# Weight scaling cut into slices on two engines, v stored in blocks, and two reorderings around the output projection of a gMLP and attention trunk

## The chip, the cores and the metric

The kernel runs on one core of a Trainium2 chip. The metric is the device time of one launch in microseconds; lower is better. TensorE (PE) multiplies, VectorE (DVE), ScalarE (ACT) and GpSimd (POOL) work elementwise, and SyncE (SP) issues most of the DMA transfers. ScalarE issues some too. Each engine takes its instructions strictly in order, and so does each engine's queue of DMA issues.

## The reference

The input x is 1024 tokens by 1024 channels in float32. Layer one is a gated MLP with a spatial gate, layer two a banded attention with sinks; both have a residual and a norm on each side.

```python
# layer one (gmlp_mixer), h = rms_norm(x, a_pre_g)
u, v, z = split(h @ w_in, 3)              # each 1024 x 2048
u = gelu(u); v = layer_norm(gelu(v), ln_g, ln_b)
s = einsum('gts,bnsgc->bntgc', tril(w_s), v) + b_s     # 8 groups, chunks of 128 tokens
y = (u * s * silu(z)) @ w_out             # 2048 -> 1024
h1 = x + rms_norm(y, a_post_g)
k, v = rms_norm(h1, kv_norm_g) @ w_k, ... @ w_v        # shared, 4 heads of 64
# layer two (swa_mixer), h = rms_norm(h1, b_pre_g)
q, z = split(h @ b_w_in, 2)               # 16 heads of 64
o = softmax(q k^T + alibi, sliding window 128, sink) v
out = h1 + rms_norm((o * silu(z)) @ b_w_out, b_post_g)
```

## The kernel before

Every large product is taken as three matmuls of 128x128 by 128x512 on operands split in a high and a low part: hi*hi, hi*lo and lo*hi (`mm3`, the profile's lines L174 to L176). `split` (L104) makes the parts: ScalarE copies the high part (L105), VectorE subtracts it (L106). So each weight or activation piece passes ScalarE and then VectorE before TensorE can take it.

The stages follow one another on TensorE, in this order and at these times of the span: `v_layer` (0 to some 163 us; steps m = 1, 2, 5, 6, 7, 4, 3 for two halves Q of the columns, banks vb and vc), `uz_layer` (to 482; banks ub, uc, ua, the spatial gate from vg and wc), `out_layer` (to 658; seven products m, four steps u each, banks ob and oc), `q_phase` of token half 0 (to 702), `kv_phase` (to 725), `z_phase` of half 0 (to 775), attention of half 0 (to 905), and the other half with the last projection. The first three layers use a scheme of seven products for a 2x2 block product, so a bank is added to several results and some are reused: in `out_layer` the bank oc takes m=5 and, right behind it, m=3.

The code is written as Python generators; a `side` generator is advanced by `step(side)` between groups of matmuls, so that norms and transposes run beside the matmuls. The order in which instructions are issued within an engine is then set by a scheduler that starts from the order written. What a table of orders shows below is the result.

The parts that the change touches:
- `Weights.split` (L133) prepares the 40 weight tiles of layer two, each 128x1024. The 16 of kind "q" (w_q and w_z of the first half) are first multiplied by the gain b_pre_g, in place, by one GpSimd instruction over the whole tile (L144); then split, and the scaled tile is written back to DRAM by ScalarE's queue (`wsc`, L151), from where the second half reads it without scaling.
- `v_layer` applies GELU to each 128x512 tile of v (`done`, L387) and `emit` (L381) takes its statistics on VectorE and stores the tile, 256 KB, to `vd` in DRAM, one store issued by ScalarE behind each activation.
- `out_layer` (L767): at the end of a product m each of the four token tiles t is summed with the bank (`add`, L211, yoa<-yoa,oc), and `done` (L844) takes its sum of squares on ScalarE (junk_oa, L188) and multiplies it by the gain a_post_g on VectorE (yoa<-yoa,gpa).
- `norm_h1` (L747) norms a half of layer one's output, h1, for layer two: tile hb = h1 * r (L755), eight transposes to the banks nt (L761), split into n_hi and n_lo. For half 0 it takes yo, the tiles on chip, as a side of m=5 and m=3; for half 1 it loads h1 back from DRAM (`h1d`), four loads of 512 KB on SP, as a side of `z_phase`.
- `group_consts` (L575), unchanged, loads wc and bsb for the spatial gate of each of eight groups on SP's queue; the matmul rb (L585) needs wc, after GpSimd's affine_select (L583) has masked it.

Of the kernel before, what the change touches and what calls it, by code (L numbers as in the profile page):

```python
# [34 lines left out]
def step(*gens):  # L35
    for g in gens:
        next(g, None)
# [7 lines left out]
def drain(g):  # L45
    for _ in g:
        pass
# [3 lines left out]
def tile_yoco(  # L51
# [63 lines left out]
    class Weights:  # L115
# [17 lines left out]
        def split(self, i):  # L133
            while len(self.done) <= min(i, len(self.order) - 1):
                n = len(self.done)
                self.load(n)
                raw, (src, kind, back) = self.raw[n], self.order[n]
                hi = wpool.tile([P, 1024], F32R, tag="whi", name=f"whi{n}")
                lo = wpool.tile([P, 1024], F32R, tag="wlo", name=f"wlo{n}")
                halves = [slice(kk * 512, kk * 512 + 512) for kk in range(2)]  # L140
                if kind == "q":
                    rv = raw.rearrange("p (k c) -> p k c", k=KT)
                    g = gn[:, G_BPRE:G_BPRE + KT].unsqueeze(2).broadcast_to([P, KT, P])
                    nc.gpsimd.tensor_tensor(rv, rv, g, ALU.mult)  # L144
                if kind[:2] == "kv":
                    for kk, cs in enumerate(halves):
                        split_scaled(hi[:, cs], lo[:, cs], raw[:, cs], gain(G_KV, 2 * int(kind[2:]) + kk))
                else:
                    split(hi, lo, raw)
                if back is not None:  # L150
                    nc.scalar.dma_start(out=back, in_=raw)  # L151
                self.done.append((hi, lo))
# [10 lines left out]
    def gain(c, k):  # L163
        return gn[:, c + k:c + k + 1]
# [25 lines left out]
    def load_tok(src, name):  # L190
        t = st.tile([P, D], F32, tag="xt", name=name)
        nc.sync.dma_start(out=t, in_=src)
        return t
# [100 lines left out]
    def v_layer(ahead):  # L294
# [83 lines left out]

        stats = vp.tile([P, NB, 4, 6], F32, name="bst")

        def emit(slot_, i, j, t, Q):  # L381
            qd = 2 * Q + i
            nc.vector.bn_stats(stats[:, 4 * j + t, qd], slot_)
            nc.scalar.dma_start(out=vd[4 * j + t, :, qd * 512:(qd + 1) * 512], in_=slot_)

        def done(out, src, i, j, t, Q):
            nc.scalar.activation(out, src, AF.Gelu_apprx_tanh, scale=rx[j][:, t:t + 1])  # L387
            emit(out, i, j, t, Q)

        ORDER = (1, 2, 5, 6, 7, 4, 3)  # L390
        steps = [(Q, m, u) for Q in range(2) for m in ORDER for u in range(2)]
# [42 lines left out]
        for n, (Q, m, u) in enumerate(steps):  # L434
            if u == 0:
                if m == 1:
                    bank_b = [bank("mm", f"vb{Q}_{t}") for t in range(4)]
                elif m in (2, 5):
                    bank_c = [bank("s", f"vc{Q}{m}_{t}") for t in range(4)]
            ps = bank_b if m in (1, 6, 7, 4) else bank_c  # L440
            first = m in (1, 2, 5)
            hi, lo = ready.pop(n)
            for kk in range(2):
                k = 2 * u + kk
                cs = slice(kk * 512, kk * 512 + 512)
                for t in range(4):
                    ts_ = slice(t * P, (t + 1) * P)
                    mm3(ps[t], T[m][0][:, k, ts_], T[m][1][:, k, ts_], hi[:, cs], lo[:, cs],
                        first and k == 0, k == HT - 1)
            if n >= 2:  # L450
                prep(n + 2)
            if n >= len(steps) - 3:
                step(ahead)
            if n == 0:
                xload(xa[:, 1], 0, 1, 0, 2)
            elif n == 1:
                prep(3)
                xload(xa[:, 1], 0, 1, 2, 2)
            elif n >= 4:
                step(side)  # L460
            if u == 0:
                continue
            for t in range(4):
                if m == 1:
                    a1.append(slots[0][:, t])
                    copy(a1[t], ps[t])
                elif m == 2:
                    add(a1[t], a1[t], ps[t], ALU.add)
                    if Q:
                        done(a1[t], a1[t], 0, 0, t, Q)  # L470
                elif m == 6:
                    if t == 0:
                        e6 = big.tile([P, 4, TH], F32, tag="P1_3", name=f"ve6_{Q}")
                    copy(e6[:, t], ps[t])
                elif m == 7:
                    e67.append(slots[1][:, t])
                    copy(e67[t], ps[t])
                    add(e67[t], e67[t], bank_c[t], ALU.add)
                    if Q:
                        done(e67[t], e67[t], 1, 1, t, Q)  # L480
                elif m == 4:
                    c = slots[Q][:, t]
                    done(c, ps[t], 1, 0, t, Q)
                elif m == 3:
                    add(e6[:, t], e6[:, t], ps[t], ALU.add)
                    done(e6[:, t], e6[:, t], 0, 1, t, Q)

            late = {6: (a1, 0), 4: (e67, 1)}.get(m) if Q == 0 else None
            if late:
                for t in range(4):  # L490
                    done(late[0][t], late[0][t], late[1], late[1], t, Q)
            if m == 3:
                a1, e67 = [], []
            if Q == 1 and m == 2:
                broadcast_rstd()
# [248 lines left out]
        rstd(r1[h], s1, f"h1{h}")  # L744
        yield

    def norm_h1(h, n, yo=None):  # L747
        for t in range(4):
            if yo is None:
                xt = load_tok(h1d[h][t], f"hb{h}_{t}")  # L750
                src = xt
            else:
                xt = st.tile([P, D], F32, tag="xt", name=f"hb{h}_{t}")
                src = yo[t]
            nc.vector.tensor_scalar(xt, src, r1[h][:, t:t + 1], None, ALU.mult)  # L755
            yield
            for kq in range(2):
                ps = bank("s", f"nt{h}_{t}_{kq}").rearrange("p (k t) -> p k t", k=4)
                for k in range(4):
                    c = (kq * 4 + k) * P  # L760
                    nc.tensor.transpose(ps[:, k], xt[:, c:c + P], ident)  # L761
                sl = (slice(None), slice(kq * 4, kq * 4 + 4), slice(t * P, (t + 1) * P))
                split(n[0][sl], n[1][sl], ps)
            yield


    def out_layer():  # L767
# [84 lines left out]
        for n, (m, u) in enumerate(steps):  # L852
# [12 lines left out]
            for kk in range(2):  # L865
                cs = slice(kk * 512, kk * 512 + 512)
                k = 2 * u + kk
                for t in range(4):
                    ts_ = slice(kk * 512 + t * P, kk * 512 + (t + 1) * P)
                    mm3(ps[t], thi[:, ts_], tlo[:, ts_], shi[:, cs], slo[:, cs],  # L870
                        m in (1, 2, 5) and k == 0, k == 7)
                step(side)
            if u < 3:
                prep(n + 2)
                continue
            for t in range(4):
                if m == 1:
                    if t == 0:
                        yo[0] = yo_alloc((0, 1), "yoa0")
                    copy(yo[0][t][:, half[0]], ps[t])  # L880
                elif m == 2:
                    dst = yo[0][t][:, half[0]]
                    add(dst, dst, ps[t], ALU.add)
                    done(t, 0, 0, dst)
                elif m == 6:
                    if t == 0:
                        yo[1] = yo_alloc((2, 3), "yoa1")
                    copy(yo[1][t][:, half[0]], ps[t])
                elif m == 7:
                    copy(yo[1][t][:, half[1]], ps[t])  # L890
                elif m == 4:
                    evac_out(yo[0][t], ss[0], ps[t], t, 1, gp, "oa10")
                elif m == 5:
                    dst = yo[1][t][:, half[1]]
                    add(dst, dst, ps[t], ALU.add)
                    done(t, 1, 1, dst)
                else:
                    dst = yo[1][t][:, half[0]]
                    add(dst, dst, ps[t], ALU.add)
                    done(t, 0, 1, dst)  # L900
            prep(n + 2)
            if m == 4:
                n0 = pair("P3", "n0")
                side = chain(chain_a(0, yo[0], ss[0], xs), iter(range(2)), norm_h1(0, n0, yo[0]))
# [270 lines left out]
    for _ in main:  # L1175
        step(side)
    drain(side)
    gp = post_gain(b_post, "gpb")
    drain(kv_phase(0, n0))
    n1 = pair("P2", "n1")  # L1180
    z0, z1 = ([big.tile([P, 4, TH], F32, tag=f"P1_{2 * i}", name=f"z{h}_{i}") for i in range(2)]
              for h in range(NH))
    side = norm_h1(1, n1)
    for _ in z_phase(0, n0, z0, 0, 8):
        step(side)
    drain(side)
# [74 lines left out]
```

## Time and profile before

| | before |
|---|---|
| median of 3 runs | 1063.02 us (1061.49 to 1063.05) |
| the profiled execution | 1062.77 us |
| its span | 1061.1 us |
| TensorE busy | 1045.5 us, 5114 matmuls |
| VectorE / ScalarE / GpSimd busy | 739.6 / 569.5 / 233.0 us |
| DMA moved | 168.08 MB |

Rows of the profile read as follows. A row of the timeline begins with its start and its length in us; then come the engine, the line, the operation, output<-inputs with the buffer numbers left out, shapes, a count, and in brackets the idle time ahead of it on its engine and what ended it. ACTq and SPq are the issuing of transfers. A row of the waits tells who waited for whom: us in total, how many times, the longest. A row of a group has the busy time and the mean ns of one, then the idle time ahead of the group and its releasers. A DMA row ends in the median us from issue to landing. A 128x512 matmul is listed with 0.39 us, but the next starts 0.23 us later, since they overlap.

### The profile page before, as it was taken

How to read it: one execution, taken by the hardware profiler on the slowest of the kernel's cores; microseconds unless marked ns; L12 is line 12 of the kernel's file. 1: busy time of each engine (PE TensorE's matmuls, PEld its weight loads, DVE VectorE, ACT ScalarE, POOL GpSimd, SP SyncE). 2: the span in 40 equal slices, each digit the busy share in tenths (PEclk: the TensorE clock that was granted, in tenths of full speed). 3: DMA queues.
4: the chain of work that ended last, by engine and by line, in shares of the span. 5: the costliest groups of instructions: out<-in, count | busy, mean ns of one | idle time of the engine just before them, and what ended most of it. 6: DMA issues, size and time to landing. Idle time of an engine off the chain costs nothing.

```text
span 1061.1 us, 14120 instructions
## 1 busy us (share of the span) xinstructions
PE 1045.5 (99%) x5114; PEld 857.0 (81%) x5114; DVE 739.6 (70%) x1292; ACT 569.5 (54%) x973; POOL 233.0 (22%) x197
## 2 busy tenths in 40 slices
PE   9999999999999999999999989999999999999997
PEld 7887788888888888888888878788887777777776
DVE  6987466867767768678696586755357885667963
ACT  6674454555564555464444463544456665766631
POOL 0000003254253442540100121303101111122320
PEclk9999999999999999999999999999999999999999
DMA  8777252434333434348997643846522112111353
GB/s 311 265 276 262 99 177 91 131 112 135 115 109 129 139 103 132 115 141 281 344 331 255 218 159 129 288 152 219 175 72 71 62 61 80 61 60 61 120 179 119
DMA packets 70871, 168.08 MB, mean 158 GB/s; under 512 B 6417, under 2 KB 16913, under 8 KB 70801
## 3 DMA queue, kind: packets, MB, share of 16 engines
q1 hardware_dynamic: 63456, 150.04, 41.6%
q10 hardware_dynamic: 7344, 17.14, 4.3%
q8 instruction: 40, 0.66, 0.2%
q14 instruction: 31, 0.25, 0.1%
HBM read 127.31 MB, written 39.85 MB: 158 GB/s over the span
## 4 chain that ended last, share of the span: by engine, by line
PE 84%; DVE 6%; ACT 3%; DMA 3%; issue 2%; POOL 1%; ACTq 0%; DVEq 0%; POOLq 0%; SPq 0%
PE ub L174 5%; PE ub L176 5%; PE ub L175 5%; PE ob L174 5%; PE ob L176 5%; PE ob L175 5%; PE qz L174 5%; PE qz L176 5%; PE qz L175 5%; PE uc L175 3%; PE uc L174 3%; PE uc L176 3%; PE sp L602 3%; PE vb L175 2%; PE vb L176 2%
## 5 line engine op out<-in xcount | busy, mean ns | idle before, releaser
L174 PE MATMUL qz<-n_hi,whi 128*128 128x512 f32 x256 | 102.1, 399 | 0.4 <-DVE kl L994 0.2
L176 PE MATMUL qz<-n_hi,wlo 128*128 128x512 f32 x256 | 100.1, 391 | 1.1 <-DVE wlo L106 1.1
L175 PE MATMUL qz<-n_lo,whi 128*128 128x512 f32 x256 | 99.7, 390 | 0.0
L106 DVE TENSOR_TENSOR wlo<-raw_w,whi 128x1024 fp32r<-128x1024 f32 x40 | 51.7, 1292 | 42.9 <-ACT whi L105 30.1
L144 POOL TENSOR_TENSOR raw_w<-raw_w,gn 128x1024 f32<-128x1024 f32 x16 | 35.4, 2215 | 189.9 <-DMA raw_w<-in_wqz_dram 172.0
L1040 ACT ACTIVATE pr<-pr,mx 128x129 f32<-128x129 f32 x128 | 50.0, 393 | 36.4 <-DVE mx L1035 36.4
L105 ACT ACTIVATE whi<-raw_w 128x1024 fp32r<-128x1024 f32 x40 | 42.3, 1057 | 41.2 <-PE qz L175 19.7
L105 ACT ACTIVATE uzhilo_g<-f 128x1024 fp32r<-128x1024 f32 x31 | 32.8, 1060 | 48.0 <-PE uc L176 43.0
L176 PEld LDWEIGHTS qz<-n_hi,wlo 128*128 128x128 f32 x256 | 48.0, 188 | 12.2 <-DVE wlo L106 1.8
L174 PEld LDWEIGHTS qz<-n_hi,whi 128*128 128x128 f32 x256 | 48.1, 188 | 10.4 <-issue 0.8
L1059 POOL TENSOR_SCALAR_AFFINE_SELECT pp<-pc 128x512 f32<-128x512 f32 x28 | 20.5, 733 | 163.4 <-ACT pc L1056 163.4
L175 PEld LDWEIGHTS qz<-n_lo,whi 128*128 128x128 f32 x256 | 48.2, 188 | 9.4
L214 ACT ACTIVATE uz_slots<-ub 128x512 f32<-128x512 f32 x48 | 28.4, 591 | 43.6 <-PE ub L176 41.5
L106 DVE TENSOR_TENSOR uzhilo_g<-f,uzhilo_g 128x1024 fp32r<-128x1024 f32 x31 | 38.6, 1246 | 18.7 <-ACT uzhilo_g L105 18.6
L174 PE MATMUL ub<-T,whi_g 128*128 128x512 f32 x128 | 50.6, 396 | 0.0
L174 PE MATMUL ub<-T,uzhilo_g 128*128 128x512 f32 x128 | 50.5, 394 | 0.0
L176 PE MATMUL ub<-T,wlo_g 128*128 128x512 f32 x128 | 49.9, 390 | 0.0
L176 PE MATMUL ub<-T,uzhilo_g 128*128 128x512 f32 x128 | 49.9, 390 | 0.0
L175 PE MATMUL ub<-T,uzhilo_g 128*128 128x512 f32 x128 | 49.8, 389 | 0.0
L175 PE MATMUL ub<-T,whi_g 128*128 128x512 f32 x128 | 49.8, 389 | 0.0
L174 PE MATMUL uc<-T,uzhilo_g 128*128 128x512 f32 x124 | 48.9, 395 | 0.0
L175 PE MATMUL uc<-T,uzhilo_g 128*128 128x512 f32 x124 | 48.3, 389 | 0.0
(328 smaller groups left out, 3158.3 us busy)
## 6 DMA issues: line engine op xcount, KB each, us to landing
raw_uz<-in_wuz_in_dram SPq DMA_DIRECT2D x32, 512.0 KB, 3.5
td<-uz_slots SPq DMA_DIRECT2D x56, 256.0 KB, 2.1
orawP2a<-td SPq DMA_DIRECT2D x28, 512.0 KB, 4.1
raw<-in_wv_in_dram SPq DMA_DIRECT2D x17, 512.0 KB, 5.2
vg<-vd SPq DMA_DIRECT2D x8, 1024.0 KB, 5.4
orawP2b<-in_wo_a_dram SPq DMA_DIRECT2D x16, 512.0 KB, 8.0
raw_w<-in_wqz_dram SPq DMA_DIRECT2D x16, 512.0 KB, 4.2
wsc<-raw_w ACTq DMA_DIRECT2D x16, 512.0 KB, 3.0
```

Source lines behind the costliest of these rows:

```text
L105: nc.scalar.activation(hi, src, AF.Copy)
L106: nc.vector.tensor_tensor(lo, src, hi.bitcast(F32), ALU.subtract)
L144: nc.gpsimd.tensor_tensor(rv, rv, g, ALU.mult)
L174: nc.tensor.matmul(out, lhsT=a_hi, rhs=b_hi, start=start, stop=False, skip_group_check=True)
L175: nc.tensor.matmul(out, lhsT=a_hi, rhs=b_lo, start=False, stop=False, skip_group_check=True)
L176: nc.tensor.matmul(out, lhsT=a_lo, rhs=b_hi, start=False, stop=stop, skip_group_check=True)
L214: nc.scalar.activation(out, a, AF.Copy)
L602: nc.tensor.matmul(psv[:, n], lhsT=d["vg"][:, 4 * j + n, i * P:(i + 1) * P], rhs=d["wc"], start=True, stop=True)
L1040: nc.scalar.activation(pr[:, i], pr[:, i], AF.Exp, bias=mx[:, i // 2, i % 2:i % 2 + 1], scale=-1.0, accum_out=dn[:, i // 2, i % 2:i % 2 + 1])
L1059: nc.gpsimd.affine_select(self.pp, pc, [[0, 4], [-1, P]], ALU.is_ge, 0.0, base=-1, channel_multiplier=1)
```

## The change

Four edits.
1. The 16 weight tiles of kind "q" are scaled in eight slices of 128x128, each by its own column of gains: two slices on ScalarE (new line L146), six on GpSimd (L148).
2. A block of four token tiles of v is stored by one transfer of 1 MB instead of four of 256 KB, issued behind all four activations: 8 stores instead of 32, on the same queue.
3. In `out_layer` the four sums of m=5 are written ahead of their squares and products by gpa, and the last advance of the side generator in a product's last step comes after the evacuation, not before it (twice then, so that the number stays).
4. `norm_h1` of half 1 takes the tiles on chip like half 0, starts in the q phase of half 0 and goes on in `z_phase`; the four loads from `h1d` are gone, and the tile pair n1 is taken earlier. The stores to `h1d` stay, since the last residual reads them.

```diff
 # Weights.split
-                    g = gn[:, G_BPRE:G_BPRE + KT].unsqueeze(2).broadcast_to([P, KT, P])
-                    nc.gpsimd.tensor_tensor(rv, rv, g, ALU.mult)
+                    for k in range(KT):
+                        g = gain(G_BPRE, k)
+                        if k < 2:
+                            nc.scalar.activation(rv[:, k], rv[:, k], AF.Copy, scale=g)
+                        else:
+                            nc.gpsimd.tensor_scalar(rv[:, k], rv[:, k], g, None, ALU.mult)
 # v_layer
-        def emit(slot_, i, j, t, Q):
-            qd = 2 * Q + i
-            nc.vector.bn_stats(stats[:, 4 * j + t, qd], slot_)
-            nc.scalar.dma_start(out=vd[4 * j + t, :, qd * 512:(qd + 1) * 512], in_=slot_)
+        def store(block, i, j, Q):
+            dst = vd[4 * j:4 * j + 4, :, (2 * Q + i) * 512:(2 * Q + i + 1) * 512]
+            nc.scalar.dma_start(out=dst.rearrange("n p c -> p n c"), in_=block)
 
         def done(out, src, i, j, t, Q):
             nc.scalar.activation(out, src, AF.Gelu_apprx_tanh, scale=rx[j][:, t:t + 1])
-            emit(out, i, j, t, Q)
+            nc.vector.bn_stats(stats[:, 4 * j + t, 2 * Q + i], out)
...
+            block = {3: (e6, 0, 1), 4: (slots[Q], 1, 0)}.get(m)
+            if Q and m in (2, 7):
+                block = (slots[0], 0, 0) if m == 2 else (slots[1], 1, 1)
+            if block:
+                store(*block, Q)
...
                 for t in range(4):
                     done(late[0][t], late[0][t], late[1], late[1], t, Q)
+                store(slots[late[1]], late[1], late[1], Q)
 # norm_h1
-    def norm_h1(h, n, yo=None):
+    def norm_h1(h, n, yo):
         for t in range(4):
-            if yo is None:
-                xt = load_tok(h1d[h][t], f"hb{h}_{t}")
-                src = xt
-            else:
-                xt = st.tile([P, D], F32, tag="xt", name=f"hb{h}_{t}")
-                src = yo[t]
-            nc.vector.tensor_scalar(xt, src, r1[h][:, t:t + 1], None, ALU.mult)
+            xt = st.tile([P, D], F32, tag="xt", name=f"hb{h}_{t}")
+            nc.vector.tensor_scalar(xt, yo[t], r1[h][:, t:t + 1], None, ALU.mult)
 # out_layer
-                step(side)
+                if u < 3:
+                    step(side)
...
                     dst = yo[1][t][:, half[1]]
                     add(dst, dst, ps[t], ALU.add)
-                    done(t, 1, 1, dst)
...
             prep(n + 2)
+            if m == 5:
+                for t in range(4):
+                    done(t, 1, 1, yo[1][t][:, half[1]])
+            step(side, side)
 # behind the q phase of half 0
+    n1 = pair("P2", "n1")
+    side = norm_h1(1, n1, yo)
+    step(side)
     drain(kv_phase(0, n0))
-    n1 = pair("P2", "n1")
...
-    side = norm_h1(1, n1)
```

Lines behind the first edit move by 4, those behind `v_layer`'s by 10. The new order at three places, where a name's first part is the tile and the number behind it its serial:

SP's queue at the end of `v_layer`, where the loads for the first quads of `uz_layer` (raw_uz) and the constants of group 0 (vg, wc, bsb) go out; before:

```order
L101 DMA raw_uz_0_1364<-in_wuz_in_dram 128x1024
L578 DMA vg_1351<-vd 128x8x256
L101 DMA raw_uz_1_1366<-in_wuz_in_dram 128x1024
L580 DMA wc_1353<-in_ws_t_dram 128x128
L582 DMA bsb_1355<-in_bs_dram 128x128
L580 DMA wc_1631<-in_ws_t_dram 128x128
```

and with the change:

```order
L101 DMA raw_uz_0_1340<-in_wuz_in_dram 128x1024
L588 DMA vg_1327<-vd 128x8x256
L101 DMA raw_uz_1_1342<-in_wuz_in_dram 128x1024
L101 DMA raw_uz_0_1427<-in_wuz_in_dram 128x1024
L590 DMA wc_1329<-in_ws_t_dram 128x128
L592 DMA bsb_1331<-in_bs_dram 128x128
```

The third load of a raw_uz_0 has moved ahead of wc and bsb; its buffer is free when VectorE has split the piece wlo_g_1 of the load before it.

VectorE between m=5 and m=3, where yoa_2 holds token tiles 0 and 1 and yoa_3 tiles 2 and 3, oc_0 to oc_3 are the four banks, and gpa is the gain; before:

```order
L211 TENSOR_TENSOR yoa_2_4305<-yoa_2_4305,oc_0_4606 128x512
L211 TENSOR_TENSOR yoa_2_4305<-yoa_2_4305,oc_1_4607 128x512
L211 TENSOR_TENSOR yoa_3_4306<-yoa_3_4306,oc_2_4608 128x512
L211 TENSOR_TENSOR yoa_2_4305<-yoa_2_4305,gpa 128x512 x2
L211 TENSOR_TENSOR yoa_3_4306<-yoa_3_4306,oc_3_4609 128x512
L211 TENSOR_TENSOR yoa_3_4306<-yoa_3_4306,gpa 128x512
```

and with the change:

```order
L215 TENSOR_TENSOR yoa_2_4281<-yoa_2_4281,oc_0_4582 128x512
L215 TENSOR_TENSOR yoa_2_4281<-yoa_2_4281,oc_1_4583 128x512
L215 TENSOR_TENSOR yoa_3_4282<-yoa_3_4282,oc_2_4584 128x512
L215 TENSOR_TENSOR yoa_2_4281<-yoa_2_4281,gpa 128x512
L215 TENSOR_TENSOR yoa_3_4282<-yoa_3_4282,oc_3_4585 128x512
L215 TENSOR_TENSOR yoa_2_4281<-yoa_2_4281,gpa 128x512
L215 TENSOR_TENSOR yoa_3_4282<-yoa_3_4282,gpa 128x512
```

The fourth sum (oc_3) has moved ahead of the second product by gpa, not of the first.

TensorE around the end of m=3, where nt_3 are the transposes of token tile 3 of half 0 and qz_0_0 the first q product; before:

```order
L174 MATMUL oc_3_4609<-ohiloP0b,ohiloP0a 128x512
L175 MATMUL oc_3_4609<-ohiloP0b,ohiloP0a 128x512
L176 MATMUL oc_3_4609<-ohiloP0b,ohiloP0a 128x512
L761 MATMUL nt_3_0_4929<-ident,hb_3_4915 128x128 x4
L761 MATMUL nt_3_1_4936<-ident,hb_3_4915 128x128 x4
L174 MATMUL oc_0_4606<-ohiloP0b,ohiloP0a 128x512
L175 MATMUL oc_0_4606<-ohiloP0b,ohiloP0a 128x512
L176 MATMUL oc_0_4606<-ohiloP0b,ohiloP0a 128x512
```

and, further on there, up to the q phase:

```order
L175 MATMUL oc_2_4608<-ohiloP0b,ohiloP0a 128x512
L176 MATMUL oc_2_4608<-ohiloP0b,ohiloP0a 128x512
L174 MATMUL oc_3_4609<-ohiloP0b,ohiloP0a 128x512
L175 MATMUL oc_3_4609<-ohiloP0b,ohiloP0a 128x512
L176 MATMUL oc_3_4609<-ohiloP0b,ohiloP0a 128x512
L174 MATMUL qz_0_0_5006<-n_hi,whi_4992 128x512
L175 MATMUL qz_0_0_5006<-n_lo,whi_4992 128x512
L176 MATMUL qz_0_0_5006<-n_hi,wlo_4993 128x512
```

With the change:

```order
L180 MATMUL oc_2_4584<-ohiloP0b,ohiloP0a 128x512
L178 MATMUL oc_3_4585<-ohiloP0b,ohiloP0a 128x512
L179 MATMUL oc_3_4585<-ohiloP0b,ohiloP0a 128x512
L180 MATMUL oc_3_4585<-ohiloP0b,ohiloP0a 128x512
L766 MATMUL nt_3_0_4933<-ident,hb_3_4891 128x128 x4
L766 MATMUL nt_3_1_4940<-ident,hb_3_4891 128x128 x4
L178 MATMUL qz_0_0_4996<-n_hi,whi_4968 128x512
L178 MATMUL qz_0_1_5057<-n_hi,whi_4981 128x512
L179 MATMUL qz_0_0_4996<-n_lo,whi_4968 128x512
L180 MATMUL qz_0_0_4996<-n_hi,wlo_4969 128x512
```

The transposes have moved behind the last oc matmul, right ahead of the first matmuls that read the n_hi and n_lo made from them. A matmul of the second q product has come between.

ScalarE at the same place, where whi is a weight's high part, wsc_3 the store of the next scaled weight, and junk_oa the squares; before:

```order
L105 ACTIVATE whi_4992<-raw_w_4871 128x1024
L105 ACTIVATE n_hi<-nt_2_0_4889 128x4x128
L105 ACTIVATE n_hi<-nt_2_1_4896 128x4x128
L105 ACTIVATE whi_4998<-raw_w_4873 128x1024
L151 DMA wsc_3_91<-raw_w_5004 128x1024
L105 ACTIVATE n_hi<-nt_3_0_4929 128x4x128
L105 ACTIVATE n_hi<-nt_3_1_4936 128x4x128
L188 ACTIVATE junk_oa_0_4956,ssa_3859<-yoa_2_4305 128x512
L151 DMA wsc_4_92<-raw_w_5058 128x1024
L188 ACTIVATE junk_oa_1_4960,ssa_3859<-yoa_2_4305 128x512
```

and with the change:

```order
L105 ACTIVATE n_hi<-nt_2_1_4872 128x4x128
L146 ACTIVATE raw_w_4994<-raw_w_4994,gn 128x128 x2
L155 DMA wsc_3_91<-raw_w_4994 128x1024
L105 ACTIVATE whi_4981<-raw_w_4849 128x1024
L192 ACTIVATE junk_oa_0_4918,ssa_3835<-yoa_2_4281 128x512
L192 ACTIVATE junk_oa_1_4922,ssa_3835<-yoa_2_4281 128x512
L105 ACTIVATE n_hi<-nt_3_0_4933 128x4x128
L192 ACTIVATE junk_oa_2_4926,ssa_3835<-yoa_3_4282 128x512
L105 ACTIVATE n_hi<-nt_3_1_4940 128x4x128
L146 ACTIVATE raw_w_5055<-raw_w_5055,gn 128x128
L192 ACTIVATE junk_oa_3_4930,ssa_3835<-yoa_3_4282 128x512
```

The two slices and wsc_3 now stand ahead of whi_4981, and n_hi of tile 3 behind two squares. On VectorE all four sums and three of the four products by gpa stand ahead of the first n_lo<-nt_3.

## The prediction

> **What bounds the kernel now.** I read the busy table first, then the waits of TensorE, then the timeline around each wait. The page's head:
>
> ```profile
> span 1061.1 us, 14120 instructions
> PE 1045.5 (99%) x5114; PEld 857.0 (81%) x5114; DVE 739.6 (70%) x1292; ACT 569.5 (54%) x973; POOL 233.0 (22%) x197
> PEclk9999999999999999999999999999999999999999
> ```
>
> TensorE is busy for 99% of the span at a full granted clock. The change gives it the same matmuls in another order, so only its idle time can shrink or grow. The waits of TensorE (who, for whom: total us, times, longest):
>
> ```profile
> PE oc L174 <- DVE yoa L211: 2.8, 2, 1.9
> PE nt L761 <- DVE hb L755: 1.4, 1, 1.4
> PE qz L176 <- DVE wlo L106: 1.1, 1, 1.1
> PE vb L175 <- DVE vlo L106: 0.8, 1, 0.8
> ```
>
> That is 6.1 us, and the other rows of the view are the start-up and 0.4 or less each. What the change can win is therefore at most these 6.1; what it can lose has no such bound. The profiled execution took 1062.77 us, 0.25 under the median of 1063.02; the sum is made against the former.
>
> **Stores of v in blocks.** In v_layer's step m=4 ScalarE issues each 256 KB store between two activations:
>
> ```profile
> 79.73 1.68 ACTq L384 DMA_DIRECT2D vd<-vslot  x2
> 81.47 1.06 ACT L105 ACTIVATE vhi<-vraw 128x1024 fp32r<-128x1024 f32 x1 [1.14 <-issue]
> 83.88 1.07 PE L174 MATMUL vb<-vhi,T 128*128 128x512 f32 x4
> 83.24 1.26 DVE L211 TENSOR_TENSOR ve<-ve,vc 128x512 f32<-128x512 f32 x2
> 84.43 1.22 DVE L106 TENSOR_TENSOR vlo<-vraw,vhi 128x1024 fp32r<-128x1024 f32 x1
> ```
>
> Two issues take 1.68 there, and vhi starts late behind them. One issue per four tiles moves vhi to about 80, and VectorE's new order puts vlo ahead of the sums with vc: vlo can end between 81 and 83.7, and TensorE, one matmul every 0.23 us, wants it after its four of 83.88, at 84.8. **-0.8**. A slot of 1 MB comes free later than four of 256 KB; that could hold ScalarE for a microsecond or two at 150, where TensorE has no wait in 100 us. Nothing.
>
> **Order at uz_layer's start.** SP's order now puts the load raw_uz_0, which needs the piece that VectorE splits at the end of v_layer, ahead of group 0's wc:
>
> ```profile
> 156.62 0.47 SPq L580 DMA_DIRECT2D wc<-in_ws_t_dram  x1
> wc<-in_ws_t_dram SPq DMA_DIRECT2D x2, 64.0 KB, 3.7
> wc<-in_ws_t_dram SPq DMA_DIRECT2D x8, 64.0 KB, 5.2
> 166.93 0.17 DVE L498 TENSOR_SCALAR ve<-mv 128x8 f32<-128x8 f32 x1
> 167.17 1.64 POOL L499 TENSOR_TENSOR ve<-ve,small 128x8 f32<-128x8 f32 x1 [1.52 <-DVE ve L498]
> 168.78 0.64 POOL L583 TENSOR_SCALAR_AFFINE_SELECT wc<-wc 128x128 f32<-128x128 f32 x2
> 169.69 0.38 PE L585 MATMUL rb<-wc,ones 128*128 128x128 f32 x2
> ```
>
> Before, wc went out at 156.6 and lay ready nine us before rb. Now the piece wlo_g_1, which stands about where ve<-mv does, ends near 167.1, wc goes out at 167.5 and lands 3.7 later (the first two here) or 5.2 (median of all eight), at 171.2 to 172.7; affine_select 0.3. TensorE reaches rb ten matmuls (2.3 us) later in its new order and 0.9 earlier by the gain above: 171.0. **+0.5**, bounds 0 and 2.
>
> **Sums of the reused bank in out_layer, m=5 to m=3, and the slices there.**
>
> ```profile
> 627.55 3.95 POOL L144 TENSOR_TENSOR raw_w<-raw_w,gn 128x1024 f32<-128x1024 f32 x1 [3.79 <-DMA raw_w<-in_wqz_dram]
> 628.52 1.22 DVE L106 TENSOR_TENSOR wlo_s<-scho,whi_s 128x1024 fp32r<-128x1024 f32 x1
> 629.66 1.87 DVE L211 TENSOR_TENSOR yoa<-yoa,oc 128x512 f32<-128x512 f32 x3
> 631.53 0.33 ACTq L151 DMA_DIRECT2D wsc<-raw_w  x1
> 631.96 0.63 ACT L188 ACTIVATE junk_oa<-yoa 128x512 bf16<-128x512 f32 x1 [5.97 <-DVE yoa L211]
> 632.71 1.45 DVE L211 TENSOR_TENSOR yoa<-yoa,gpa 128x512 f32<-128x512 f32 x2 [1.18 <-ACT junk_oa L188]
> 634.08 0.68 DVE L211 TENSOR_TENSOR yoa<-yoa,oc 128x512 f32<-128x512 f32 x1
> ```
>
> The reading is a chain: POOL's scaling ends at 631.50, only then does ScalarE issue the store wsc, then the squares (junk_oa) of tile 0 and 1, then VectorE multiplies both by gpa, and only then comes the fourth sum (634.08), for which TensorE waits 1.9. The new order does not do all that its words say: one product by gpa still stands ahead of the fourth sum. It removes one, 0.7. What a slice costs no row shows; the nearest:
>
> ```profile
> L583 POOL TENSOR_SCALAR_AFFINE_SELECT wc<-wc 128x128 f32<-128x128 f32 x8 | 2.4, 306 | 12.3 <-PE ub L176 7.9 <-DMA wc<-in_ws_t_dram 4.5
> L211 POOL TENSOR_TENSOR f<-raw_uz,raw_uz 128x512 f32<-128x512 f32 x15 | 19.2, 1282 | 125.6 <-DVE uzhilo_g L106 125.6
> L1040 ACT ACTIVATE pr<-pr,mx 128x129 f32<-128x129 f32 x128 | 50.0, 393 | 36.4 <-DVE mx L1035 36.4
> 651.72 1.90 POOL L144 TENSOR_TENSOR raw_w<-raw_w,gn 128x1024 f32<-128x1024 f32 x1 [20.22 <-DMA raw_w<-in_wqz_dram]
> ```
>
> ScalarE's two: 0.4 each. POOL's: affine_select has the same shape and one input, 0.3, so six take 1.8; the line through the two TENSOR_TENSOR (1282 ns for 512, 1.90 for 1024) gives 0.66 + 1.2 ns per element, 0.82 at 128, and six take 4.9. I take 1.8, since one operand is a column. The 3.95 at 627.55 is 2.05 more than 1.90, and 627.55 + 2.11 is just where wlo_s gave way to the sums at 629.66: the scaling waited out VectorE's two-input instructions. If the slices wait as long, they end at 631.4 and the gain is 0.7 plus 0.1 to 0.3: **-1.0**; if they slip in earlier, up to -1.9. The other wait of this pair, 0.9, stands behind wlo_s and stays.
>
> The Trainium skill (SBUF — State Buffer, "SBUF: two separate sides") says that VectorE with two SBUF inputs and GpSimd exclude each other for a whole instruction, and whoever starts first holds the ports. The 3.95 agrees. By that rule six short instructions could lose the ports six times, which speaks against the change; at 628 only wlo_s is left to lose to, so the sum by the rule stays at -1.0, and without it would be -1.9.
>
> **The last transposes, moved behind the last sums of m=3.**
>
> ```profile
> 652.06 1.06 ACT L105 ACTIVATE whi<-raw_w 128x1024 fp32r<-128x1024 f32 x1 [2.15 <-issue]
> 654.53 1.03 PE L761 MATMUL nt<-ident,hb 128*128 128x128 f32 x8
> 655.17 1.09 ACT L105 ACTIVATE n_hi<-nt 128x512 fp32r<-128x512 f32 x2 [2.05 <-PE nt L761]
> 657.00 1.87 DVE L211 TENSOR_TENSOR yoa<-yoa,oc 128x512 f32<-128x512 f32 x3
> 657.91 0.39 PE L176 MATMUL oc<-ohiloP0b,ohiloP0a 128*128 128x512 f32 x1
> 658.14 0.39 PE L174 MATMUL qz<-n_hi,whi 128*128 128x512 f32 x1
> ```
>
> Before, tile 3 of the normed half was transposed at 654.5, and its n_hi and n_lo were ready before the q phase began at 658.1. Now the eight transposes follow the last oc matmul, and the first q matmul needs n_hi, the third n_lo. In times of after (1.0 earlier here, and the 0.8 of the moved transposes comes off the sums too): the oc matmuls are through at 656.4, the transposes at 657.2. ScalarE: two slices and wsc of the next weight (landed 650.8, POOL done 652.6) stand ahead of whi, which so ends at 653.9; wlo follows to 655.0, the sums 0 to 2 to 656.9; junk of tiles 0 and 1 to 657.3; n_hi 657.9. First q matmul 657.9 instead of 657.2: 0.6. VectorE: products 0 and 1 to 658.1, sum 3 to 658.7, product 2 to 659.3, then n_lo to 659.9. The two matmuls with n_hi alone end their turn at 658.4: 1.6 more. **+2.2**. Below, 0.6 if the products slip behind n_lo's data; above, 3.1 more, if the six slices take 4.9, since whi waits for wsc.
>
> **What goes behind it.** The wait at 669 (1.1 for wlo) had this cause:
>
> ```profile
> 662.45 2.21 DVE L211 TENSOR_TENSOR yoa<-yoa,gpa 128x512 f32<-128x512 f32 x3 [2.38 <-ACT junk_oa L188]
> 669.41 1.23 DVE L106 TENSOR_TENSOR wlo<-raw_w,whi 128x1024 fp32r<-128x1024 f32 x1
> ```
>
> The norm of the second half, two instructions of VectorE ahead of this wlo, hangs on the last product by gpa, which now ends at 661 instead of 664.7. wlo ends near 668.8, and TensorE, 1 late, wants it at 670.8. **-1.1**. Later VectorE's hb of the second half stands ahead of a q_hi and a wlo and waits for POOL's r behind six slices: 0 to 1, **+0.3**.
>
> **The second half normed from tiles on chip.** The wait at 737 follows a load of 512 KB that SP issues late:
>
> ```profile
> 731.15 3.13 SPq L725 DMA_DIRECT2D hb<-h1d  x2
> 736.96 0.39 PE L176 MATMUL qz<-n_hi,wlo 128*128 128x512 f32 x1
> ```
>
> Without the four loads hb needs yo and r only, both ready some 40 us earlier. **-1.4**. The tiles P1_2 and P1_3 stay taken longer; z0 waits for hb of tiles 0 and 1, which are done in the q phase.
>
> Sum: -0.8 + 0.5 - 1.0 + 2.2 - 1.1 + 0.3 - 1.4 = -1.3, so 1062.77 - 1.3 = 1061.5. Differences under 0.2% (2.1 us) can't be told from no change here, so 1060.9 to 1065.1 counts as the same.
>
> **Rivals.**
> 1. The q phase starts without its stall (products late, n_lo early) and all four waits go whole: -0.8 - 1.9 - 1.1 - 1.4 + 0.6 = -4.6, 1058.2. For it: VectorE has 70% busy and its idle 2.38 us before 662.45 show room. Against it: the written order has n_lo behind three products.
> 2. Slower: a slice on POOL costs 0.8 whatever its size. Then wsc holds ScalarE at 632 (slices end 634.6, the fourth sum 3.2 later than forecast, or 1.1 if VectorE doesn't hold POOL) and at 656 (3.1 later): 1061.5 + 4.2 to 6.3, some 1066.5. It ends above the time before from 0.4 a slice, where six cost 0.6 more and that twice; against it affine_select's 306 ns.
> 3. wc takes 5.2 and rb waits 2.2: 1063.2.
> 4. The reorder does nothing, as all waits merely move to the next late operand: 1062.8.
>
> **How the numbers follow.** Forecast 0.42 (1060.0 to 1063.2, a quarter of it under 1060.9), rival 1 0.26, rival 2 0.16 (three quarters of it above 1065.1), rivals 3 and 4 0.16 together. Faster by over 0.2%: 0.11 + 0.26 = 0.37, rounded to 0.38; slower 0.12 and 0.02 from the tail of rival 3: 0.14; same 0.48. The range reaches from rival 1 without its 0.6 (1057.6) to the middle of rival 2 (1066.0) and leaves out some 0.07 below and 0.08 above.
>
> **What would show it.** In the profile after: no wait of vb for vlo, none of nt for hb; the oc wait for yoa with a longest near 0.9; a wait of qz for n_lo of some 1.6 at 658 and of qz for n_hi of 0.6; one of rb of 0.5 at 171; POOL's L148 x96 at 300 ns and ScalarE's L146 x32 at 400. The prediction is wrong if L148's mean is above 400 ns, if qz shows no wait at the start of its phase, or if another engine's wait of over a microsecond appears in a stage that I called free.

## The result, and the profile after

The changed kernel takes 1079.08 us (median of 5 runs, 1077.62 to 1080.06) against 1062.74 before: a ratio of 1.0156 with a 95% interval of 1.0141 to 1.0171. It is slower by 16.3 us, where 1061.5 was forecast. The profiled span is 1078.1 against 1061.1.

The page of the changed kernel, its head and the group that now stands first:

```profile
span 1078.1 us, 14186 instructions
PE 1054.3 (98%) x5114; PEld 862.7 (80%) x5114; DVE 734.8 (68%) x1292; ACT 578.8 (54%) x1005; POOL 265.2 (25%) x277
L148 POOL TENSOR_SCALAR raw_w<-raw_w,gn 128x128 f32<-128x128 f32 x96 | 68.7, 734 | 178.9 <-DVE ohiloP0b L106 90.7
```

TensorE has the same 5114 matmuls, but is busy 8.8 us longer: some of them ran slower. The rest is idle time. Two of the prediction's signs of being wrong are here: the slices (L148) have a mean of 734 ns, over 400, and a wait of over a microsecond stands at the start of the z phase (behind vt, 2.2), a place that was called free. The waits of TensorE after:

```profile
PE oc L178 <- DVE yoa L215: 5.2, 2, 2.8
PE qz L178 <- DVE vt L1005: 2.2, 1, 2.2
PE qz L178 <- ACT n_hi L105: 2.2, 1, 2.2
PE rb L595 <- POOL wc L593: 2.1, 1, 2.1
PE qz L180 <- DVE wlo L106: 1.4, 3, 0.6
PE qz L179 <- DVE n_lo L106: 1.1, 1, 1.1
PE oc L179 <- DVE wlo_s L106: 0.9, 1, 0.9
```

Two of the four waits of before are gone (vb for vlo, nt for hb), as forecast. New ones stand at rb, at the start of the q phase and at the start of the z phase, and those of oc have doubled. Where 17.0 us of span went, counted from the starts of neighbouring matmuls less the 0.23 us that an undisturbed one takes:

| place | before | after |
|---|---|---|
| v_layer, vb for vlo | 0.9 | 0 |
| uz_layer, rb for wc (171) | 0 | 2.3 |
| out_layer, oc between m=5 and m=3 (627 to 641) | 3.2 | 6.5 |
| q phase, its start (666 to 670) | 0 | 3.8 |
| q phase, wlo | 1.2 | 1.4 |
| z phase, its start (741) and nt for hb | 1.9 | 2.4 |
| z phase, wlo (765) | 0 | 0.5 |
| slow matmuls behind the waits | 0 | 6.7 |
| sum | 7.2 | 23.6 |

The difference, 16.4, is all but 0.6 of the 17.0. Three places of the profile after show the chain. GpSimd, ScalarE and VectorE between m=5 and m=3:

```profile
632.90 5.70 POOL L148 TENSOR_SCALAR raw_w<-raw_w,gn 128x128 f32<-128x128 f32 x6 [3.67 <-DMA raw_w<-in_wqz_dram]
638.63 0.33 ACTq L155 DMA_DIRECT2D wsc<-raw_w  x1
639.00 0.63 ACT L192 ACTIVATE junk_oa<-yoa 128x512 bf16<-128x512 f32 x1 [5.58 <-POOL raw_w L148]
639.76 0.69 DVE L215 TENSOR_TENSOR yoa<-yoa,gpa 128x512 f32<-128x512 f32 x1 [2.74 <-ACT junk_oa L192]
640.37 0.68 DVE L215 TENSOR_TENSOR yoa<-yoa,oc 128x512 f32<-128x512 f32 x1
```

Six slices take 5.70 us; wsc, the first square, the product and the fourth sum follow one another behind them. ScalarE at the end of kv_phase, where kh takes the bank that the z phase needs:

```profile
740.42 0.33 ACTq L155 DMA_DIRECT2D wsc<-raw_w  x1
740.79 0.59 ACT L1002 ACTIVATE kh<-pk 64x512 fp32r<-64x512 f32 x1 [3.93 <-POOL raw_w L148]
```

The store of a scaled z weight stands ahead of kh in ScalarE's queue and waits 3.9 for GpSimd. And TensorE at the start of the q phase:

```profile
668.49 1.15 PE L178 MATMUL qz<-n_hi,whi 128*128 128x512 f32 x2 [2.16 <-ACT n_hi L105]
670.70 0.79 PE L179 MATMUL qz<-n_lo,whi 128*128 128x512 f32 x1 [1.05 <-DVE n_lo L106]
671.29 0.63 PE L180 MATMUL qz<-n_hi,wlo 128*128 128x512 f32 x1
671.72 0.63 PE L178 MATMUL qz<-n_hi,whi 128*128 128x512 f32 x1
```

Behind the waits a matmul takes 0.63 and starts every 0.43 us, for some 4 us. The granted clock of this stretch:

```profile
664.00:668.00 4.00, 2.33 (x15) 1.80 (x13) 3.38 (x5) 2.08 (x6) 0.00 (x0) 1.00 0.61 193
668.00:672.00 4.00, 2.46 (x5) 1.54 (x6) 4.00 (x8) 2.84 (x8) 2.28 (x4) 0.57 0.50 201
672.00:676.00 4.00, 4.00 (x12) 3.10 (x12) 1.58 (x4) 0.02 (x1) 2.63 (x4) 0.57 0.69 262
676.00:680.00 4.00, 4.00 (x19) 3.34 (x18) 1.77 (x2) 3.81 (x6) 0.00 (x0) 1.00 0.81 293
```

Behind the stretch and its length stand the busy times of PE, PEld, DVE, ACT and POOL, then PEclk, the DMA share and GB/s. PEclk is 0.57 over these 8 us and 1.00 on both sides; from 668.60 to 675.42 alone it is 0.50.

### The profile page after: what moved, and what is told of

Same layout as the page of the kernel before. It is cut to its first block, busy times and chain, and to the rows that moved or that the text cites. A ratio compares the mean times of both kernels' runs of the same rounds, so it can differ in the third digit from the quotient of the medians.

```text
span 1078.1 us, 14186 instructions
## 1 busy us (share of the span) xinstructions
PE 1054.3 (98%) x5114; PEld 862.7 (80%) x5114; DVE 734.8 (68%) x1292; ACT 578.8 (54%) x1005; POOL 265.2 (25%) x277
## 5 line engine op out<-in xcount | busy, mean ns | idle before, releaser
L148 POOL TENSOR_SCALAR raw_w<-raw_w,gn 128x128 f32<-128x128 f32 x96 | 68.7, 734 | 178.9 <-DVE ohiloP0b L106 90.7
L215 POOL TENSOR_TENSOR f<-raw_uz 128x512 f32<-128x512 f32 x15 | 19.4, 1296 | 129.2 <-DMA raw_uz<-in_wuz_in_dram 99.2
L105 ACT ACTIVATE whi_g<-raw_uz 128x1024 fp32r<-128x1024 f32 (+1 forms) x31 | 26.5, 855 | 45.3 <-PE ua L179 23.7
```

Of the source, the lines that this page charges most:

```text
L105: nc.scalar.activation(hi, src, AF.Copy)
L148: nc.gpsimd.tensor_scalar(rv[:, k], rv[:, k], g, None, ALU.mult)
L215: (eng or nc.vector).tensor_tensor(out, a, b, op)
```

## The experiments

Theory A: the slices on GpSimd are dear, and wsc, the squares, whi and kh wait behind them. Theory B: the new orders are at fault, whoever scales. Two kernels part them, two more look at rb and at the engine that scales. They ran on one chip against 1063.29 before.

**Slices undone**

```diff
-                    for k in range(KT):
-                        g = gain(G_BPRE, k)
...
-                            nc.gpsimd.tensor_scalar(rv[:, k], rv[:, k], g, None, ALU.mult)
+                    g = gn[:, G_BPRE:G_BPRE + KT].unsqueeze(2).broadcast_to([P, KT, P])
+                    nc.gpsimd.tensor_tensor(rv, rv, g, ALU.mult)
```

> The changed kernel with each weight tile scaled by one GpSimd instruction again; all else as changed, and TensorE's and SP's orders are the same as in the changed kernel. Theory A (the slices: 0.60 us each on GpSimd plus what VectorE holds it up, 3.5 to 5.7 for six against 1.9 to 3.9 whole, so that wsc, the squares and whi wait behind them): the waits of oc for yoa fall from 5.2 to about 2, that of qz behind kv_phase (2.2) goes, those at the start of the q phase shrink by about 2, and two or three of the four stretches of slow clock with them; 1079.1 - 11 = about 1068. What is left above the time before is rb's wait with its slow stretch (3.9) and about 2 at the q phase. Theory B (the new orders are at fault, the moved transposes and rb, whoever scales): 1076 or more, with the waits at the q phase and their slow clock as they are.

1063.86 us, ratio 1.0008 (0.9997 to 1.0019). Of 16 us some 15 are gone, more than A's estimate, and B falls. Its waits:

```profile
PE oc L174 <- DVE yoa L211: 2.2, 2, 1.3
PE rb L591 <- POOL wc L589: 1.8, 1, 1.8
PE qz L175 <- DVE n_lo L106: 0.8, 1, 0.8
PE qz L176 <- DVE wlo L106: 0.7, 1, 0.7
PE qz L174 <- ACT n_hi L105: 0.7, 1, 0.7
```

The wait behind kv_phase is gone, those of oc and at the q phase's start are small, and no slow stretch followed any of them.

**Slices alone**, the kernel before with this edit only:

> The kernel before with the slices alone (two on ScalarE, six on GpSimd). TensorE's order is that of before. Theory A: the waits of oc for yoa grow by 2 to 3 each and the kv phase's end waits 2 more, with one to three stretches of slow clock of about 1.5 each: 1062.7 + 8 to 12, about 1072. Theory B: within 2 us of 1062.7.

1078.62 us, ratio 1.0144 (1.0124 to 1.0163): the slices alone make the whole loss, and more than expected.

```profile
PE oc L178 <- DVE yoa L215: 5.3, 2, 2.9
PE qz L178 <- DVE vt L999: 2.2, 1, 2.2
PE qz L178 <- DVE yoa L215: 2.0, 1, 2.0
PE qz L178 <- ACT whi L105: 1.6, 1, 1.6
PE nt L765 <- DVE hb L759: 1.4, 1, 1.4
```

TensorE's order is that of before, and yet the oc and kv waits are those of the changed kernel, and the q phase waits at its start (2.0) without the moved transposes. The run also shows why the first of the two oc waits grew (by starts from 1.0 to 2.6). GpSimd's second scaling of out_layer and its next instruction, before and in this run:

```profile
604.98 2.69 POOL L144 TENSOR_TENSOR raw_w<-raw_w,gn 128x1024 f32<-128x1024 f32 x1 [3.00 <-DVE ohiloP0a L106]
614.38 1.02 POOL L184 TENSOR_TENSOR rpa<-rpa,small 128x4 f32<-128x4 f32 x1 [6.71 <-DVE rpa L183]
```

```profile
604.54 5.30 POOL L148 TENSOR_SCALAR raw_w<-raw_w,gn 128x128 f32<-128x128 f32 x6 [0.92 <-issue]
616.55 1.04 POOL L188 TENSOR_TENSOR rpa<-rpa,small 128x4 f32<-128x4 f32 x1 [6.71 <-DVE rpa L187]
```

The scaling ends 2.17 us later (609.84 for 607.67), and the wsc behind it holds the squares, the products by gpa and the norm factor rpa in the same way; GpSimd gets rpa 6.71 us behind its scaling in both. hb then starts 2.19 later on VectorE (625.98 for 623.79), and the sums that free the bank 2.29 later (631.95 for 629.66).

**wc early**: group 0's wc in a tile of its own, loaded with uz_layer's first weights.

```diff
+        wc0 = uv.tile([P, P], F32, tag="wc0", name="wc0")
+        nc.sync.dma_start(out=wc0, in_=ws_t[:, 0])
         fetch(0)
```

> The changed kernel with group 0's wc loaded into a tile of its own some 100 us earlier, so that rb doesn't wait for it; TensorE's order near rb moves a little. If the stretch of slow clock behind rb's wait (8 matmuls at 0.43 instead of 0.23 us, 1.5 lost) comes from that wait: both go, 1079.1 - 3.7 = 1075.4. If the slow stretch is something of its own: only the wait goes, 1076.9, and the slow matmuls stay near 174.

1076.81 us (1074.66 to 1077.77), ratio 1.0119 (1.0094 to 1.0145). The windows of 170 to 180 us, of the changed kernel and of this one:

```profile
170.00:180.00 10.00, 7.91 (x29) 6.00 (x28) 4.01 (x11) 2.26 (x4) 0.58 (x2) 0.83 0.17 34
```

```profile
170.00:180.00 10.00, 9.79 (x43) 7.76 (x42) 7.55 (x15) 2.88 (x5) 3.32 (x4) 1.00 0.37 120
```

rb's wait and the slow clock behind it (0.83) both go. The median fell by 2.3, between the two expectations; in the profile a longer wait in v_layer (1.2 instead of 0.4) and a slightly longer start of the q phase ate some of it.

**All eight slices on ScalarE**, in the changed kernel:

```diff
-                        if k < 2:
-                            nc.scalar.activation(rv[:, k], rv[:, k], AF.Copy, scale=g)
-                        else:
-                            nc.gpsimd.tensor_scalar(rv[:, k], rv[:, k], g, None, ALU.mult)
+                        nc.scalar.activation(rv[:, k], rv[:, k], AF.Copy, scale=g)
```

> The changed kernel with all eight slices of a tile on ScalarE (0.39 us each, 3.1 for a tile) and none on GpSimd. Theory A as a matter of GpSimd's duration: the scaling then takes 3.1 without VectorE in its way, the oc waits lose 2 to 3 in all and the kv wait goes: 1070 to 1073. If it is instead that any slice in ScalarE's queue holds the squares and whi up: no gain, 1078 or more, since 3.1 of ScalarE's own time stands in the queue where 0.8 stood.

1060.50 us, ratio 0.9969 (0.9958 to 0.9979): faster than before, and some 10 below what A expected: the oc waits and the one at the z phase's start went whole, and the slow clock behind them. Only rb's wait with its slow stretch and 0.8 and 1.1 at the q phase's start are left.

The next four: why a slice is dear, and what is best. They ran against 1063.34 before.

**One instruction for six slices**, over 128x768 with one column of gains, so that five column blocks have the wrong gain:

```diff
-                            nc.gpsimd.tensor_scalar(rv[:, k], rv[:, k], g, None, ALU.mult)
+                    nc.gpsimd.tensor_scalar(raw[:, 256:1024], raw[:, 256:1024], gain(G_BPRE, 2), None, ALU.mult)
```

> The changed kernel, but GpSimd scales its six columns by one instruction over 128x768 with a single column of gains, where six had their own (so the q and z weights have wrong gains; orders on the other engines are unchanged). If a slice's 0.60 us is mostly a cost per instruction: one instruction takes 1.0 to 1.5, the time falls to that with the whole tile on GpSimd or below, 1061 to 1064. If it is a cost per element of this operation (4.5 ns each): 3.5 again, and the time stays near 1079.

1071.38 us, ratio 1.0081 (1.0066 to 1.0097), between the two. The instructions, min/median/max in ns, of the changed kernel and of this one:

```profile
L148 POOL TENSOR_SCALAR raw_w<-raw_w,gn x96: 596/603/2802, 602.1 to 776.5; 128x128 f32<-128x128 f32 x96
```

```profile
L145 POOL TENSOR_SCALAR raw_w<-raw_w,gn x16: 2206/2210/4372, 600.9 to 762.6; 128x768 f32<-128x768 f32 x16
```

Undisturbed, 0.60 for 128 elements and 2.21 for 768: the line through both gives 0.28 us an instruction and 2.5 ns an element. Neither expectation alone is right; six slices pay 1.7 for being six and 1.9 for their elements, and even one instruction is dearer than the whole tile as TENSOR_TENSOR (1.90). So 0.3 us more on GpSimd, with two slices on ScalarE, still cost 7.5 us against the whole tile: by starts 3.3 at oc (2.5 with the whole tile), 3.4 at the start of the q phase (1.8), 3.2 at that of the z phase (0.3), and two slow stretches, 3.0 (none). At the q phase the order on ScalarE has a part in it: with slices wsc stands ahead of whi, and whi, at 656.47, waits 2.01 for GpSimd; with the whole tile whi goes first, at 652.24, and wsc at 654.54. At the z phase's start GpSimd itself waited 4.95 for the load of the weight (729.49). Why that load came so late is not shown.

**ScalarE alone**: the kernel before with eight slices on ScalarE and nothing else changed.

> The kernel before with the scaling alone changed, to eight slices on ScalarE and none on GpSimd; its order of sums, its loads of hb and its stores of v stay. If ScalarE's slices by themselves take the waits at 632 and 669 (3.0 of the 6.1): 1062.7 - 2 to 3 = about 1060. If they gain only together with the sums written first: 1062.2 to 1063.

1056.02 us (1055.78 to 1057.21), ratio 0.9935 (0.9923 to 0.9948): 7 us faster than before, 4 more than expected, since the first oc wait (1.0) and that of nt for hb (1.6) went too, although hb is still loaded from DRAM (its loads go out at 725.40, 731.15 before). The span is 7.0 shorter, more than the 6.1 that the prediction took for the most that could be won. All waits of TensorE over 0.4 but the start-up and vb's are gone:

```profile
PE warm L911 <- DVE small L93: 1.1, 1, 1.1
PE vb L175 <- DVE vlo L106: 0.8, 1, 0.8
PE vb L175 <- DVE wlo_v L420: 0.4, 1, 0.4
```

ScalarE and VectorE at the reused bank:

```profile
626.05 2.43 ACT L144 ACTIVATE raw_w<-raw_w,gn 128x128 f32<-128x128 f32 x8
628.51 0.33 ACTq L151 DMA_DIRECT2D wsc<-raw_w  x1
628.89 0.63 ACT L188 ACTIVATE junk_oa<-yoa 128x512 bf16<-128x512 f32 x1 [0.40 <-DVE yoa L211]
628.16 2.47 DVE L211 TENSOR_TENSOR yoa<-yoa,oc 128x512 f32<-128x512 f32 x4
```

Eight slices take 2.43, 0.30 each, wait for no other engine, and are done before the squares could start. All four sums now run first (x4), though the code has them as before.

**ScalarE and wc early**, in the changed kernel:

> All slices on ScalarE and wc loaded early, all else as in the changed kernel. rb's wait (2.2) and the slow stretch behind it (1.6) were still there at 1060.5: both gone gives 1056.7; only the wait gone, 1058.3. An unchanged 1060.5 would mean that the place of rb in TensorE's order costs the same in another way.

1057.77 us (1057.02 to 1058.34), ratio 0.9949 (0.9936 to 0.9961). rb's wait and its slow stretch are gone in the profile; against the 1060.5 without wc early that is 2.7, where 3.8 was counted.

**The same with the transposes where they were**:

```diff
-                if u < 3:
-                    step(side)
+                step(side)
...
-            step(side, side)
```

> The same, with the side generator advanced where it was before, so that tile 3's transposes stand ahead of the last oc matmuls again. The waits at the start of the q phase (0.8 + 1.1) go: 1.9 less than the run without this, 1054.9. If the place of the transposes is not what makes these waits, but the norm's squares and products on ScalarE and VectorE are late anyway: no difference.

1055.97 us (1055.90 to 1056.25), ratio 0.9933 (0.9921 to 0.9946): 1.8 less, the waits at the start of the q phase are gone. So beside ScalarE's scaling the moved transposes cost 1.8, and stores, sums, tiles and an early wc on top of the scaling on ScalarE are no better than that scaling alone.

**The other edits alone**, each the change's own lines for that part put into the kernel before, on a chip that scattered more (before: 1064.24, 1061.24 to 1066.84). Stores of v in blocks:

> The kernel before with v's stores in blocks alone. SP's order at the start of uz_layer is then that of the changed kernel, with a raw_uz ahead of wc. As the runs so far read: vb's wait for vlo goes (-0.9), rb waits 2.0 to 2.3 for wc, with or without 1.5 of slow clock behind it: 1062.7 + 1.1 to 2.7, about 1064.5. If the reorder came from another edit: 1061.8 and no wait of rb.

1064.97, ratio 1.0011 (1.0002 to 1.0021). vb's wait is gone, rb waits 2.2 for wc with 1.6 of slow clock behind; the reorder of SP comes from this edit. This profile and the next three each have one more slow stretch, of some 1.6, which the first profile of the kernel before did not have: behind an oc wait here, in the run with tiles and in the last, and behind nt's wait in the run with sums.

```profile
PE rb L591 <- POOL wc L589: 2.2, 1, 2.2
```

The second half normed from the tiles on chip:

> The kernel before with the second half normed from the tiles on chip alone. The prediction's term: the wait of nt for hb (1.4, 1.6 by starts) goes and nothing comes in its place: 1061.2. If a later operand is as late (n_hi and n_lo of the same tiles, or whi behind wsc): within 0.5 of 1062.7.

1064.78, ratio 1.0005 (0.9991 to 1.0018). The wait of nt for hb (1.6 by starts) is gone, but in the q phase the waits for wlo, behind hb on VectorE, grow from 1.2 to 2.3 by starts:

```profile
PE qz L176 <- DVE wlo L106: 2.0, 2, 1.8
```

The sums of m=5 first:

> The kernel before with the sums of m=5 written first, alone; VectorE's order has the fourth sum one place earlier, behind one product by gpa. The prediction's term without the slices: one product less, 0.7 of the second oc wait: 1062.0. If the scheduler's order decides nothing here because the squares are late: 1062.7.

1062.95, ratio 0.9986 (0.9976 to 0.9997). The oc waits fall from 2.8 to 2.1, 0.7 as expected.

```profile
PE oc L174 <- DVE yoa L211: 2.1, 2, 1.3
```

Whole-tile scaling on GpSimd, stores, sums and tiles, without the moved transposes:

> The changed kernel with the whole-tile scaling on GpSimd again and the side generator advanced where it was before, so only stores, sums and tiles are changed. Against the run with the move (1063.9, where the q phase started with waits of 0.9 and 1.0 by starts): if the moved transposes cost what was predicted (2.2): 1061.9. If the wait at 669 for wlo (1.1) then comes back: 1063.

1065.57, ratio 1.0010 (1.0000 to 1.0020), within its scatter of the run with the move, though the q phase starts without a wait: the profile has 1.2 for wlo back at 672, another 1.9 at 684 (0.9 with the move), and 2.8 in one oc wait, beside rb's 2.3. So beside GpSimd's scaling the moved transposes saved behind the start of the q phase about what they cost there.

**The slow stretches.** 6.7 of the 17 us are slow matmuls. Three profiles more, of kernels that had one already, ask whether they belong to the program.

> The kernel before, profiled again. If the slow stretch comes and goes between executions: the same waits (2.1 in out_layer, 1.2 and 1.6 later), of which one or another now has slow matmuls behind it, with a span 1.0 to 1.7 longer per stretch. If it hangs on the program: none, as in the first profile, and a span within 0.5 of 1061.1.

> The kernel before a third time. If the slow stretch comes and goes between executions, one of the two further profiles should show one behind a wait of 1.2 to 2.1; if it hangs on the program, neither.

> The changed kernel, profiled again. If the slow stretches come and go: the same waits, with three to five stretches that need not stand at the same four waits (171, 638, 666, 741). If they hang on the program: the same four.

They took 1064.96, 1062.76 and 1078.42 us. The kernel before has its second oc wait, 2.1 us by starts, in both of its profiles, with a slow stretch behind it in one (span 1063.2) and none in the other (1061.0). The changed kernel's second profile kept three of its four; the one behind rb's 2.2 was missing. So such a stretch comes and goes between executions.

The traces show what it hangs on. A stretch has a clock of 0.50 for 3.41 us, or for twice that, and the stretches of one execution lie on a grid: those of the changed kernel begin at 173.66, 641.29, 668.60 and 743.69, which are 137.0, 8.0 and 22.0 times 3.413 us apart. The place of the grid differs from one execution to the next. The second profile of the kernel before, the window of its grid with the wait in it and the next one:

```profile
633.58:636.99 3.41, 1.51 (x10) 1.26 (x10) 3.07 (x5) 3.41 (x7) 0.00 (x0) 1.00 0.25 96
636.99:640.40 3.41, 3.41 (x11) 2.73 (x10) 3.41 (x5) 1.26 (x4) 0.00 (x0) 0.50 0.00 0
```

and the third, where the grid (taken from the stretch at the span's end) cuts the same wait in two:

```profile
630.45:633.86 3.41, 2.42 (x10) 1.75 (x10) 2.17 (x4) 1.83 (x5) 1.09 (x1) 1.00 0.40 156
633.86:637.27 3.41, 2.42 (x14) 2.12 (x15) 3.14 (x5) 3.41 (x8) 0.00 (x0) 1.00 0.01 2
```

In the first TensorE is idle (3.41 less PE's busy time) for 1.90 us of one window, in the second for 0.99 of each of two. Over the windows of all 17 traces (from 20 us to 1000 us) in which the clock was full: with 1.95 us or more of idle time in one window, the next was slow in all 19; with 1.90 to 1.93, in four of six; with 1.76 or less, in none.

## Why the prediction was wrong, step by step

- **The price of a slice on GpSimd: wrong, and the largest single step.** The prediction took 1.8 for six from affine_select (0.3 each) and kept 4.9 (0.82 each) as the other end. Measured were 0.60 undisturbed, 0.73 in the mean, 3.5 to 5.7 for six: twice the price taken, and nearer to the two-input row than to the row of its own shape. Why it is so dear is not shown. With the price near the forecast, 2.21 in the run with one instruction, 1071.4 was measured, so the price itself accounts for some 7.7 of the 17.6 us between 1061.5 and 1079.1.
- **What hangs on a scaling: only in part counted.** The other ten lie in waits where the sum had nothing or too little, and the run with one instruction has them still. The sum put nothing at the start of the z phase, where kh waits for wsc (2.1 more than before), and held the first oc wait for fixed behind wlo_s ("stays"), though it hangs on the scaling 25 us ahead through wsc, the squares, rpa and hb, and grew from 1.0 to 2.5. Rival 2 was the right mechanism, decided from 0.4 a slice and placed wsc at 632 and 656, but its 1066.5 was 12.6 short, since it left out these two and the slow clock. (Two small slips beside it: the middle of its own sum, 4.2 to 6.3 over 1061.5, is 1066.8, not the 1066.0 that ends the range; and rival 3's wait of 2.2 is 2.0 by the prediction's own times, 173.0 less 171.0.)
- **The slow clock: not in the sum.** Every wait was priced at its own length. Waits of 1.7 to 3.1 us had some 1.6 of slow matmuls behind them in many executions, 6.7 in all here. The Trainium skill (TensorE: Matmul & The Clock Gate, "What's actually happening") tells of an activity window of 3413 ns that runs free of the program, with half the clock after an idle one. The trace agrees with half speed (0.43 against 0.23 us), with 3.41 us per stretch, with the grid and with its coming and going; but the windows ahead of a stretch were not idle throughout here, 1.90 us of idle time in one were enough in some.
- **rb and wc: mechanism right, size off.** 0.5 was taken, with 3.7 for the landing. In the timeline after, wc went out when forecast, but landed 5.5 later, so the wait was 2.3, above the bound of 2, plus some 1.6 of slow clock. Why the landing took so long is not shown:

```profile
167.17 0.70 SPq L590 DMA_DIRECT2D wc<-in_ws_t_dram  x1
172.71 0.60 POOL L593 TENSOR_SCALAR_AFFINE_SELECT wc<-wc 128x128 f32<-128x128 f32 x2 [3.96 <-DMA wc<-in_ws_t_dram]
```

- **Stores of v in blocks: right on its own term**, -0.9 against -0.8. With rb's wait the edit is a small loss (1064.97 against 1064.24).
- **Sums first: right.** 0.7 by one product less, in the run alone. With GpSimd's slices the second oc wait still grew, from 2.1 to 3.0.
- **The moved transposes: right at the start of the q phase.** 2.2 forecast there, 1.8 to 1.9 measured without GpSimd's slices (0.8 and 1.0 with the whole tile, 0.8 and 1.1 with ScalarE). With the slices 3.8, since whi waits for wsc, as the upper bound said.
- **669: the wait went, as forecast.** With the whole tile it came back when the move was undone (1.2 at 672), so the move and this gain belong together. **hb ahead of wlo: under-priced**, 0.3 of 0 to 1 taken, 1.9 measured at 682 in the run with tiles alone; so **the norm from the tiles** gave 1.1 of its 1.6 back there.
- **GpSimd held up by VectorE: right in kind.** At 632.90 the first slice lasted 2.80 while VectorE ran ohiloP0a and wlo_s, and ended 0.5 behind the latter; the other five took 0.60 each. The rule that the prediction weighed fits the first slice, and the loss by six lost turns did not occur there.

What stays open: what exactly TensorE must do in a window to keep its clock, since of six windows with 1.90 to 1.93 us of idle time two kept it; why a slice costs 0.60; and why loads came late, that of wc in the changed kernel and that of a z weight in the run with one instruction.

## What to carry to other kernels

An instruction that no row of the profile shows has a price only between bounds, and the row of the same shape need not be the nearest; where a few tenths of a microsecond times a queue of dependants decide the sign, the dearer end belongs in the sum. Before an operation is spread over two engines, ask what stands behind it in each queue: here the store that waited for both halves held the squares, the sums and the next weight, and the cure was to give the whole operation to the engine that the dependants stand on (ScalarE, 58% busy), which alone gained 0.65%. A wait of TensorE of two microseconds can cost nearly twice its length (2.1 and 1.6 more), or its own length alone, as it falls on the clock's windows.

## What the runs showed of the hardware

- GpSimd's TENSOR_SCALAR with a column of gains: 0.60 us for 128x128 and 2.21 for 128x768, dearer by element (2.5 ns) than TENSOR_TENSOR over 128x1024 with a broadcast operand (1.90 us in all). ScalarE's Copy with a column scale: 0.39 for 128x128, one every 0.30.
- TensorE's clock is granted at 0.50 for 3.41 us at a time, on a grid of 3.413 us whose place differs between executions. In the 17 traces a window with 1.95 us or more of idle time was always followed by such a stretch, one with 1.76 or less never. One stretch makes up some 1.6 of the 2.2 us between two profiles of the kernel before (1061.0 and 1063.2).
- GpSimd's slice waits out VectorE's instructions with two inputs: 2.80 us instead of 0.60 at 632.90, beside two of them.
